# Score matmuls over 64 rows made 128 rows by zeroed key planes, in a two-layer DiT block on one NeuronCore

## The chip, the core and the metric

The kernel runs on one core of a Trainium2 chip. The metric is device time in microseconds for one execution, the median of three runs. The core has a matrix engine (TensorE, PE in the profile, with its weight loads listed apart as PEld), a vector engine (DVE), a scalar engine (ACT), a general engine (GpSimd, POOL) and queues that issue transfers (SP). Each takes its own instructions in its own order, and they meet through semaphores.

## The reference

Two layers act on 256 image tokens x and 256 context tokens. Each layer has a feed-forward block, a token mixing and a second feed-forward block, each with a norm ahead and behind and with shift, scale and gate from a condition vector. In the second layer the context no longer gets an output of its own. What matters here is the attention inside the token mixing: 8 heads of 64 channels, with the image queries looking at image keys (with a relative bias) and at context keys, and in layer 0 the context queries at context keys.

```python
def neighbourhood_attention(q, k, v, kc, vc, rpb, rows):
    ...
    s_loc = jnp.einsum('brqhd,brkchd->bhrqkc', q, k_blk, preferred_element_type=jnp.float32) * scale
    s_loc = jnp.where(col_valid[:, None, :], s_loc + bias, NEG_INF)
    s_ctx = jnp.einsum('brqhd,bkhd->bhrqk', q, kc, preferred_element_type=jnp.float32) * scale
    ...
    p = jax.nn.softmax(scores, axis=-1).astype(v.dtype)

def context_attention(q, k, v):
    ...
    sc = jnp.einsum('bqhd,bkhd->bhqk', q, k, preferred_element_type=jnp.float32) * dh ** -0.5
```

All inputs are float32, and so is the output.

## The kernel before, in words

**Precision.** Float32 is carried through the matrix engine in pairs: an upper part rounded to the engine's float32r and a lower part, the rest. A product is three matmuls, upper by upper, upper by lower and lower by upper (`mm3`). ACT makes the upper part by a copy, DVE the lower by a subtraction (`split`).

**Weights.** `Stream` loads raw float32 weights in blocks of 1 MB through two places (`raw`) and splits them into slots of the tag `big`, of which there are 16, each 8 KB a partition. The other tags are `wk` (10 work buffers), `ps` (the 8 PSUM banks) and `st` (small statistics).

**The order.** Nothing is issued as it is written. `Recorder` takes down every operation with its operands, gives each an estimated time (`price`), and `order` lays out all engines together: an operation can run once its operands are there and its new tiles have a place, and each engine takes the one that can start first, or of several the one taken down first. A tile gets a place only if one is left for each tile asked for before it. For a matmul of float32r the price depends on the number of columns alone (lines 212 to 216), not on the rows. `issue` then issues all of it from line 376, so that every instruction of the profile has that line; the views are read by tile names instead.

**The attention.** `token_mix` goes over four pairs of heads. For each, `k_part` and `q_part` project keys (`pk`) and queries (`pq`), with two heads side by side on the 128 partitions, head 0 on the first 64 and head 1 on the others (`HEADS`). `k_evac` and `q_evac` bring them to SBUF, the image part through the rotary embedding `roped`, whose tile is `rp` and in which POOL does one of the multiplications. `kb` has the keys in three planes: plane e holds head e's upper parts on both halves of the partitions, and plane 2 holds the lower parts of both heads, each on its own half. `qa` has the queries: plane e holds head e's upper part on its own half and its lower part on the other half.

So `scores` (lines 1006 to 1008) takes two matmuls per query tile of 128 tokens. The first, over 128 rows, gives upper by upper and lower by upper at once; the second, over the 64 rows of the head, adds upper by lower:

```python
mm(ps, qa[:, e, q0 : q0 + P], kb[:, e, ks], True, False)
mm(ps, qa[hp, e, q0 : q0 + P], kb[hp, 2, ks], False, True)
```

`head` runs it for two tiles of image queries against 512 keys (bank `pS`), and in layer 0 for two tiles of context queries against 256 keys (bank `pC`). DVE takes maxima, ACT the exponentials (`sx`, `sc`), PE transposes the probabilities (`pp`), ACT and DVE split them (`pT`), and PE multiplies them with the values `v` into `po`. Between these steps the planner sets projections (`pk`, `pq`, and `pu` of the pooling branch) and, at the end, the output projection `pd`. The pooling branch (`pooled`, tiles `U`, `dd`, `ds`, `py`) runs on POOL and ends in a small matmul.

Ahead of the attention stands the end of a feed-forward block: `close` squares and sums a token tile on ACT (`sq`, then `sx` for the next norm), POOL raises the sum to the power -1/2 (`power`, tile `rs`), and DVE and ACT go on with it.

Of the kernel before, what the change touches and what calls it, by code (L numbers as in the profile page):

```python
# [17 lines left out]
P = 128  # L18
# [27 lines left out]
class Buf:  # L46
    """A logical tile; it gets one of the places of its tag while the operations that use it run."""

# [7 lines left out]
class View:  # L56
    """A part of a logical tile, with the shape arithmetic that its operations need."""

# [61 lines left out]
    def extent(self):  # L120
        """(first partition, last partition, bits of the touched groups of 32 elements)"""
        base = View.BASES[self.buf.shape]
        width = base[0].size
        off = self.shadow.__array_interface__["data"][0] - base.__array_interface__["data"][0]
        key = (off, width, self.shadow.shape, self.shadow.strides)
        if key not in View.MASKS:
            p0, f0 = divmod(off, width)
            at = np.array([f0])
            for n, st in zip(self.shadow.shape[1:], self.shadow.strides[1:]):
                if st:  # L130
                    at = (at[:, None] + st * np.arange(n)[None]).reshape(-1)
            bits = 0
            for c in np.unique(at >> 5):
                bits |= 1 << int(c)
            View.MASKS[key] = (p0, p0 + self.shadow.shape[0] - 1, bits)
        return View.MASKS[key]
# [13 lines left out]
class DramView:  # L150
    """A part of a scratch tensor in DRAM; its operations are ordered as on the whole of it."""

# [24 lines left out]
class Recorder:  # L177
    """Takes down a program of operations, orders each engine's by estimated times, and issues them so.

    An operation runs when its operands are there and its new tiles have places; of those that could run,  # L180
    the one taken down first does. A tile gets a place only if one is left for each that was asked for
    before it, up to the tag's limit."""

# [99 lines left out]
    def lag(a, b, carries):  # L283
        """Time from the end of one operation to the start of another that needs it."""
        if a.engine == b.engine:
# [7 lines left out]
    def order(self):  # L293
# [15 lines left out]
        def room(op):  # L309
            """Earliest time at which the new tiles of the operation have places, or None."""  # L310
            at, taken = 0.0, {}
# [82 lines left out]
def tile_dit_block(  # L394
# [41 lines left out]

# [1 line left out]
    ident0 = pool.tile([P, P], F32, name="ident")  # L438
# [10 lines left out]

# [1 line left out]
    class Stream:  # L451
# [86 lines left out]

# [1 line left out]
    csil = fixed([P, KD, 2], "csil")  # L540
# [59 lines left out]
    def first_mod(j):  # L600
        """Scale or shift of the first norm, on the tensor engine."""
        pr = bank("pm")
# [70 lines left out]
    def fill(n):  # L673
        """Steps of the modulation vectors of later stages, behind the work around them."""
        debt[0] += n
        rec.delay = BEHIND
        while debt[0] >= 1 and todo:
            steps = todo[0][1]
            steps.pop(0)()
            debt[0] -= 1  # L680
            if not steps:
                todo.pop(0)
        rec.delay = 0
# [4 lines left out]

# [1 line left out]
    X = [fixed([P, D], f"x{t}") for t in range(4)]  # L690
# [10 lines left out]
    def power(sq, eps):  # L701
        """(sum of the two halves' mean squares + eps) ** -0.5"""
        st = stat(2, "rs")
# [12 lines left out]
    def unit(n, x, r):  # L716
        """n = x * r, the first half on one engine and the second on another."""
        nc.vector.tensor_scalar(out=n[:, HALVES[0]], in0=x[:, HALVES[0]], scalar1=r, scalar2=None, op0=ALU.mult)
# [9 lines left out]
    def normed(t, l, jshift, n, hf, Hn, sq):  # L728
        """h = modulate(rms_norm(x)) of one token tile, transposed and split."""
        shift, scale = cols[(l, jshift)], cols[(l, jshift + 1)]  # L730
# [16 lines left out]
    def first_unit(t):  # L747
        """Normed and transposed tile of the input, in PSUM."""
        n, sq = wtile([P, D], "n"), stat(2, "sq")
# [5 lines left out]
    def first_scale(v, pts):  # L755
        """Both tiles of a stream, times the scale."""
        hf = slot([P, KD, S], "hf", F32)
# [9 lines left out]
    def first_shift(v, hf, Hn):  # L767
        """The shift, and the split."""
        tk = slice(v * S, (v + 1) * S)
# [6 lines left out]
    def close(t, pd, y, half, nxt, Hn):  # L776
        """Residual update of one token tile from its product, then the next stage's norm (or the store)."""
        n = wtile([P, D], "n")
# [47 lines left out]

# [1 line left out]
    def ffn(l, ff, both, nxt, rate, lead, parts):  # L828
# [10 lines left out]
        def product(tt, pg, pu):  # L839
            """Twice silu(gate) * up."""  # L840
            nc.scalar.activation(tt[:, 0, :], pg, AF.Tanh, scale=0.5)
# [22 lines left out]
        def by_token():  # L864
            """The first tiles with the tokens as rows, one token tile after the other."""
            wb = [ws.get() for _ in range(KD)]
# [74 lines left out]

# [1 line left out]
    def token_mix(l, nxt):  # L943
# [28 lines left out]
        def k_evac(pk, kb):  # L972
            """For each of two heads, the upper part on both halves of the partitions; then the lower parts."""
            for cs, src in ((CS, pk[:, CS]), (XS, roped(pk, 1.0))):
                for e, hp in enumerate(HEADS):
                    nc.scalar.activation(kb[hp, e, cs], src[hp], AF.Copy)
                    nc.vector.tensor_sub(kb[hp, 2, cs], src[hp], kb[hp, e, cs])
                    nc.vector.tensor_copy(kb[HEADS[1 - e], e, cs], kb[hp, e, cs])

        def q_evac(pq, qa):  # L980
            """For each of two heads, the upper part on the head's half of the partitions, the lower on the other."""
            for e, hp in enumerate(HEADS):
# [17 lines left out]
        def head(pr, e, qk, bx):  # L1000
# [5 lines left out]
            def scores(ps, q0, ks):  # L1006
                mm(ps, qa[:, e, q0 : q0 + P], kb[:, e, ks], True, False)
                mm(ps, qa[hp, e, q0 : q0 + P], kb[hp, 2, ks], False, True)

# [133 lines left out]
        columns(pq, wq, XS)  # L1143
        qk = wtile([P, 2, N_TOK], "qa", F32R), slot([P, 3, N_TOK], "kb")
        k_evac(pk, qk[1])
# [26 lines left out]
        for pr in range(4):  # L1172
# [3 lines left out]
            if pr < 3:  # L1176
                qk = wtile([P, 2, N_TOK], "qa", F32R), slot([P, 3, N_TOK], "kb")
            head(pr, 0, now, bx)
# [36 lines left out]

# [1 line left out]
    nc.sync.dma_start(out=fold, in_=foldc)  # L1217
# [34 lines left out]
def _layout(inp):  # L1252
# [4 lines left out]
    def tiles(w, cols):  # L1257
        # [K, cols*n] -> [n, 128, (K/128)*cols]
        K, W = w.shape[-2:]
# [25 lines left out]

    # bias of the relative positions, laid out by query (row parity s, column j), head, row offset, key column
    W, KH, KW = 64, 8, 16
# [61 lines left out]
```

## Time and profile before

| what | value |
|---|---|
| median of 3 runs | 1707.25 us (1706.99, 1707.25, 1710.73) |
| profiled execution, span from first to last instruction | 1708.2 us (1708.239) |
| mean granted TensorE clock | 0.990 |
| PE busy | 1662.8 us, 97% |
| DVE busy | 1133.8 us, 66% |
| ACT busy | 684.6 us, 40% |
| POOL busy | 204.1 us, 12% |
| first and last score matmul | 459.8 us (layer 0), 1481.3 us (layer 1) |

The time of the profiled execution is given by its span; the timed runs are other executions. A row of the profile reads: line, engine, operation, the tile written and the tiles read (numbers left out), shape, count, then busy time and mean duration. `64*128` ahead of a shape is the part of the array that a matmul uses, rows by columns. A row of a timeline has its start and its length first, and in brackets the idle time of the engine ahead of it and what ended it.

### The profile page before, as it was taken

What the parts mean: (1) busy time and instruction counts of PE and PEld (TensorE: products, weight loads), DVE (VectorE), ACT (ScalarE), POOL (GpSimd) and SP (SyncE); (2) the same over time, 40 slices, a digit from 0 to 9 for tenths busy, and PEclk for the clock granted to TensorE, in tenths of its full rate; (3) what the DMA queues carried; (4) which work ended last, traced back from release to release, by engine and by line L of the source; (5) the groups of instructions that cost most, each with busy time, mean ns of one, the idle gap of its engine ahead of it and who ended that gap; (6) DMA issues with size and microseconds to landing.
All of it is one profiled execution on the core that took longest, in us unless ns stands there. A gap on an engine that the chain in (4) does not pass through costs nothing.

```text
span 1708.2 us, 21855 instructions
## 1 busy us (share of the span) xinstructions
PE 1662.8 (97%) x8384; PEld 1379.1 (81%) x8384; DVE 1133.8 (66%) x1610; ACT 684.6 (40%) x1216; POOL 204.1 (12%) x248
## 2 busy tenths in 40 slices
PE   6998999999999999999999999999999999999998
PEld 4986887888877689788888888888888888779997
DVE  7978774756678769876676387623343487976664
ACT  7423222235556562223123272232222266764442
POOL 1011111101121411111110021100000022210000
PEclk9999999999999899999999999999999999999999
DMA  9477655542221435765556337722332312246551
GB/s 377 167 180 243 225 197 139 201 166 81 87 73 41 152 110 198 234 210 197 150 184 239 119 118 257 242 99 76 105 118 97 105 63 101 100 173 208 206 199 66
DMA packets 109192, 268.99 MB, mean 157 GB/s; under 512 B 19745, under 2 KB 49569, under 8 KB 97313
## 3 DMA queue, kind: packets, MB, share of 16 engines
q1 hardware_dynamic: 109088, 267.60, 46.1%
q8 instruction: 66, 1.08, 0.3%
q14 instruction: 38, 0.30, 0.1%
HBM read 251.80 MB, written 1.09 MB: 148 GB/s over the span
## 4 chain that ended last, share of the span: by engine, by line
PE 79%; DVE 7%; DMA 6%; ACT 4%; POOL 2%; issue 1%; SPq 1%; POOLq 0%; DVEq 0%; ACTq 0%
PE pd_ps L376 24%; PE pu_ps L376 22%; PE pg_ps L376 21%; DMA wm_wk<-in_wmod_dram 3%; PE pk_ps L376 2%; PE pv_ps L376 2%; ACT n_wk L376 2%; PE pq_ps L376 2%; DVE acc_wk L376 2%; POOL rs_st L376 1%; DVE w_big L376 1%; PE pS_ps L376 1%; PE po_ps L376 1%; DMA w_big<-in_wmod_dram 1%; PE pt_ps L376 1%
## 5 line engine op out<-in xcount | busy, mean ns | idle before, releaser
L376 DVE TENSOR_TENSOR w_big<-raw_raw,w_big 128x1024 fp32r<-128x1024 f32 x312 | 388.4, 1258 | 153.0 <-ACT w_big L376 152.5
L376 PE MATMUL pu_ps<-h_big,w_big 128*128 128x512 f32 (+1 forms) x2400 | 476.8, 351 | 0.1
L376 PE MATMUL pg_ps<-h_big,w_big 128*128 128x512 f32 (+1 forms) x2208 | 441.5, 354 | 1.4 <-ACT h_big L376 1.4
L376 PEld LDWEIGHTS pu_ps<-h_big,w_big 128*128 128x128 f32 x2400 | 390.1, 188 | 63.8 <-DVE w_big L376 0.3
L376 ACT ACTIVATE w_big<-raw_raw 128x1024 fp32r<-128x1024 f32 x312 | 321.8, 1053 | 298.6 <-DMA raw_raw<-in_wgu_dram 126.1
L376 PE MATMUL pd_ps<-w_big,g_big 128*128 128x512 f32 x1848 | 433.1, 395 | 1.1 <-ACT g_big L376 0.7
L376 PEld LDWEIGHTS pd_ps<-w_big,g_big 128*128 128x128 f32 x1848 | 347.2, 189 | 81.1 <-ACT g_big L376 1.2
L376 PEld LDWEIGHTS pg_ps<-h_big,w_big 128*128 128x128 f32 x2208 | 362.6, 189 | 61.9 <-ACT h_big L376 1.7
L376 DVE SCALAR_TENSOR_TENSOR acc_wk<-wm_wk,csil,acc_wk 128x1024 f32<-128x1024 f32 x196 | 249.0, 1305 | 61.8 <-DMA wm_wk<-in_wmod_dram 61.7
L376 ACT ACTIVATE g_big<-tt_wk 128x512 fp32r<-128x512 f32 (+1 forms) x84 | 49.1, 584 | 365.2 <-DVE tt_wk L376 365.2
L376 POOL TENSOR_TENSOR part_wk<-part_wk 128x512 f32<-128x512 f32 (+2 forms) x84 | 92.6, 1103 | 551.2 <-DMA part_wk<-acc_wk 464.8
L376 DVE TENSOR_TENSOR tt_wk<-tt_wk,pu_ps 128x512 f32<-128x512 f32 (+1 forms) x86 | 53.9, 627 | 59.1 <-PE pu_ps L376 58.8
L376 DVE SCALAR_TENSOR_TENSOR tt_wk<-tt_wk,pg_ps 128x512 f32<-128x512 f32 (+1 forms) x86 | 53.9, 627 | 58.4 <-ACT tt_wk L376 57.7
L376 POOL TENSOR_SCALAR rs_st<-sq_st 128x1 f32<-128x1 f32 x24 | 7.7, 321 | 705.3 <-ACT n_wk L376 705.2
L376 ACT ACTIVATE tt_wk<-pg_ps 128x512 f32<-128x512 f32 (+1 forms) x86 | 47.0, 546 | 111.6 <-PE pg_ps L376 95.9
L376 DVE TENSOR_TENSOR g_big<-tt_wk,g_big 128x512 fp32r<-128x512 f32 (+1 forms) x84 | 55.1, 656 | 42.2 <-ACT g_big L376 42.2
L376 PE MATMUL pd_ps<-w_big,mix_big 128*128 128x512 f32 x288 | 73.1, 403 | 0.0
L376 DVE TENSOR_TENSOR y_big<-y_big,pd_ps 128x512 f32<-128x512 f32 x56 | 37.4, 683 | 42.3 <-PE pd_ps L376 42.3
L376 PEld LDWEIGHTS pd_ps<-w_big,mix_big 128*128 128x128 f32 x288 | 53.3, 191 | 12.2 <-issue 0.5
L376 DVE TENSOR_SCALAR acc_wk<-wm_wk,csil 128x1024 f32<-128x1024 f32 x28 | 21.1, 770 | 56.5 <-DMA wm_wk<-in_wmod_dram 56.5
L376 PE MATMUL pk_ps<-h_big,w_big 128*128 128x512 f32 (+1 forms) x240 | 50.3, 353 | 0.0
L376 PE MATMUL pv_ps<-w_big,h_big 128*128 128x512 f32 x192 | 46.8, 396 | 0.0
(132 smaller groups left out, 1240.6 us busy)
## 6 DMA issues: line engine op xcount, KB each, us to landing
raw_raw<-in_wgu_dram SPq DMA_DIRECT2D x84, 1024.0 KB, 4.9
wm_wk<-in_wmod_dram SPq DMA_DIRECT2D x128, 512.0 KB, 6.7
raw_raw<-in_wdn_dram SPq DMA_DIRECT2D x44, 1024.0 KB, 5.1
part_wk<-acc_wk SPq DMA_DIRECT2D x224, 64.0 KB, 2.8
raw_raw<-in_wkq_dram SPq DMA_DIRECT2D x8, 1024.0 KB, 4.8
raw_raw<-in_wout_dram SPq DMA_DIRECT2D x8, 1024.0 KB, 4.9
w_big<-in_wmod_dram SPq DMA_DIRECT2D x7, 1024.0 KB, 13.5
gb_wk<-grow SPq DMA_DIRECT2D x10, 512.0 KB, 6.0
```

The costliest lines, as they stand in the source:

```text
L376: getattr(getattr(nc, op.engine), op.method)(*[self.real(a) for a in op.args], **{k: self.real(a) for k, a in op.kw.items()})
```

## The change

The key tile gets a fourth plane. Plane 2 + e now holds the lower parts of head e alone, on that head's half of the partitions, and zeros on the other half. The zeros are written by POOL, two memsets of 64 partitions by 512 columns for each pair of heads. The second matmul of `scores` then takes all 128 rows of `qa`, whose other half meets the zeros, so the sum is what it was. The tile grows from 6 to 8 KB a partition, which is the size of a place of `big`. In the diff, comments and docstrings that were emptied are left out.

```diff
         def k_evac(pk, kb):
+            for e, hp in enumerate(HEADS):
+                nc.gpsimd.memset(kb[HEADS[1 - e], 2 + e, :].bitcast(F32), 0.0)
             for cs, src in ((CS, pk[:, CS]), (XS, roped(pk, 1.0))):
                 for e, hp in enumerate(HEADS):
                     nc.scalar.activation(kb[hp, e, cs], src[hp], AF.Copy)
-                    nc.vector.tensor_sub(kb[hp, 2, cs], src[hp], kb[hp, e, cs])
+                    nc.vector.tensor_sub(kb[hp, 2 + e, cs], src[hp], kb[hp, e, cs])
                     nc.vector.tensor_copy(kb[HEADS[1 - e], e, cs], kb[hp, e, cs])
...
             def scores(ps, q0, ks):
                 mm(ps, qa[:, e, q0 : q0 + P], kb[:, e, ks], True, False)
-                mm(ps, qa[hp, e, q0 : q0 + P], kb[hp, 2, ks], False, True)
+                mm(ps, qa[:, e, q0 : q0 + P], kb[:, 2 + e, ks], False, True)
...
-        qk = wtile([P, 2, N_TOK], "qa", F32R), slot([P, 3, N_TOK], "kb")
+        qk = wtile([P, 2, N_TOK], "qa", F32R), slot([P, 4, N_TOK], "kb")
```

The last pair of lines stands at two places, lines 1144 and 1177. There are two layers of four pairs, so sixteen memsets. A memset needs no operand, so the planner can set it as soon as its tile has a place.

**POOL, end of the first feed-forward block.** Before, POOL has the powers of the last two token tiles one behind the other (`rs`: `sq` for the residual, `sx` for the next norm), and then the rotary multiplications of the attention:

```order
L376 TENSOR_TENSOR rs_st_3163<-rs_st_3163,nhalf 128x1
L376 TENSOR_SCALAR rs_st_3216<-sx_st_3195 128x1
L376 TENSOR_TENSOR rs_st_3216<-rs_st_3216,nhalf 128x1
L376 TENSOR_SCALAR rs_st_3227<-sq_st_3189 128x1
L376 TENSOR_TENSOR rs_st_3227<-rs_st_3227,nhalf 128x1
L376 TENSOR_SCALAR rs_st_3274<-sx_st_3256 128x1
L376 TENSOR_TENSOR rs_st_3274<-rs_st_3274,nhalf 128x1
L376 TENSOR_TENSOR rp_wk_3419<-rp_wk_3419,ropet 128x256
```

The same place of the changed program has the zeroing of the first two key tiles of layer 0 between them:

```order
L376 TENSOR_TENSOR rs_st_3163<-rs_st_3163,nhalf 128x1
L376 MEMSET kb_big_3198 64x512 x2
L376 TENSOR_SCALAR rs_st_3219<-sx_st_3195 128x1
L376 TENSOR_TENSOR rs_st_3219<-rs_st_3219,nhalf 128x1
L376 TENSOR_SCALAR rs_st_3230<-sq_st_3189 128x1
L376 TENSOR_TENSOR rs_st_3230<-rs_st_3230,nhalf 128x1
L376 MEMSET kb_big_3243 64x512 x2
L376 TENSOR_SCALAR rs_st_3280<-sx_st_3262 128x1
L376 TENSOR_TENSOR rs_st_3280<-rs_st_3280,nhalf 128x1
L376 TENSOR_TENSOR rp_wk_3425<-rp_wk_3425,ropet 128x256
```

Two pairs of memsets now stand ahead of a power for the next norm; the rest of POOL keeps its order there, and the other two pairs of layer 0 come further on, among the rotary and pooling steps.

**PE, first head of layer 0.** Before, the scores stand behind the values' projection `pv` and ahead of the next pair's keys `pk`:

```order
L376 MATMUL pv_ps_3499<-w_big_2983,h_big_3129 128x512
L376 MATMUL pS_ps_3536<-kb_big_3427,qa_wk_3460 128x512 x2
L376 MATMUL pS_ps_3540<-kb_big_3427,qa_wk_3460 128x512 x2
L376 MATMUL pC_ps_3546<-kb_big_3427,qa_wk_3460 128x256 x4
L376 MATMUL pk_ps_3552<-h_big_3132,w_big_3236 128x512
```

The changed program has, in the same rows of PE:

```order
L376 MATMUL pv_ps_3504<-w_big_2983,h_big_3129 128x512
L376 MATMUL pS_ps_3541<-kb_big_3198,qa_wk_3465 128x512 x2
L376 MATMUL pS_ps_3545<-kb_big_3198,qa_wk_3465 128x512 x2
L376 MATMUL pC_ps_3551<-kb_big_3198,qa_wk_3465 128x256 x4
L376 MATMUL pk_ps_3557<-h_big_3132,w_big_3239 128x512
```

Nothing has moved: in all of layer 0 PE, ACT, DVE and SP keep the order of their rows (the shape printed is that of the result, so the rows of the array that a matmul takes are not seen in it).

**POOL, pooling branch of layer 1.** Before, the steps of the second pooling group (`dd`, from `U`) follow one another:

```order
L376 TENSOR_TENSOR dd_wk_10956<-U_wk_10928 128x319
L376 TENSOR_TENSOR dd_wk_10967<-dd_wk_10956 128x317
L376 TENSOR_TENSOR dd_wk_10956<-dd_wk_10967,U_wk_10928 128x256
L376 TENSOR_TENSOR dd_wk_10956<-dd_wk_10956,U_wk_10928 128x256
L376 TENSOR_TENSOR rp_wk_11088<-rp_wk_11088,ropet 128x256
```

Now the last key tile of the layer is zeroed between them:

```order
L376 TENSOR_TENSOR dd_wk_10971<-U_wk_10943 128x319
L376 TENSOR_TENSOR dd_wk_10982<-dd_wk_10971 128x317
L376 MEMSET kb_big_10995 64x512
L376 TENSOR_TENSOR dd_wk_10971<-dd_wk_10982,U_wk_10943 128x256
L376 MEMSET kb_big_10995 64x512
L376 TENSOR_TENSOR dd_wk_10971<-dd_wk_10971,U_wk_10943 128x256
L376 TENSOR_TENSOR rp_wk_11117<-rp_wk_11117,ropet 128x256
```

The last two steps of that group stand behind a memset each. From here on the planner's order differs on PE, ACT and DVE too, in the second half of layer 1's attention and, by a row here and there, behind it.

More of the change, by code (lines that the diff above doesn't have):

```diff
@@ L1176, in token_mix @@
             if pr < 3:
-                qk = wtile([P, 2, N_TOK], "qa", F32R), slot([P, 3, N_TOK], "kb")
+                qk = wtile([P, 2, N_TOK], "qa", F32R), slot([P, 4, N_TOK], "kb")
             head(pr, 0, now, bx)
```

## The prediction

> **What bounds the kernel now.** I read the page first: which engine is full, and what the chain that ended last is made of.
>
> ```profile
> span 1708.2 us, 21855 instructions
> PE 1662.8 (97%) x8384; PEld 1379.1 (81%) x8384; DVE 1133.8 (66%) x1610; ACT 684.6 (40%) x1216; POOL 204.1 (12%) x248
> PE 79%; DVE 7%; DMA 6%; ACT 4%; POOL 2%; issue 1%; SPq 1%; POOLq 0%; DVEq 0%; ACTq 0%
> ```
>
> PE, the TensorE, is busy for 97% of the span and makes up 79% of the chain. So what shortens PE's own work counts, as long as nothing else is late instead. The change touches only the score products, so the second view is the one of the tile pS (scores of the token queries) and of pC (those of the context queries): how many of them there are, and in which shapes.
>
> ```profile
> L376 PE MATMUL pS_ps<-kb_big,qa_wk x64: 389/498/794, 459.8 to 1481.3; 128*128 128x512 f32 x32, 64*128 64x512 f32 x32
> L376 PE MATMUL pC_ps<-kb_big,qa_wk x32: 275/382/581, 461.4 to 567.9; 128*128 128x256 f32 x16, 64*128 64x256 f32 x16
> ```
>
> Half of the 96 score products run over 64 rows, 32 + 16 = 48, each recorded right behind a 128-row one. The ends of matmuls are modelled, so durations (498 ns) do not give the price; starts do. The third view is the timeline of PE, then of its weight loads, at the first head of the first layer.
>
> ```profile
> 457.42 2.50 PE L376 MATMUL pv_ps<-w_big,h_big 128*128 128x512 f32 x10
> 459.75 1.67 PE L376 MATMUL pS_ps<-kb_big,qa_wk 128*128 128x512 f32 x4
> 461.36 1.32 PE L376 MATMUL pC_ps<-kb_big,qa_wk 128*128 128x256 f32 x4
> 462.61 5.13 PE L376 MATMUL pk_ps<-h_big,w_big 128*128 128x512 f32 x21
> 467.57 0.60 PE L376 MATMUL pp_ps<-ident,sc_wk 128*128 128x128 f32 x4
> ...
> 474.06 1.46 PE L376 MATMUL po_ps<-pT_big,v_big 128*128 128x256 f32 x11
> 475.35 2.03 PE L376 MATMUL pq_ps<-h_big,w_big 128*128 128x512 f32 x8
> ```
>
> ```profile
> 459.53 0.19 PEld L376 LDWEIGHTS pS_ps<-kb_big,qa_wk 128*128 128x128 f32 x1
> 460.08 0.18 PEld L376 LDWEIGHTS pS_ps<-kb_big,qa_wk 64*128 64x128 f32 x1 [0.36 <-issue]
> ...
> 460.93 0.18 PEld L376 LDWEIGHTS pS_ps<-kb_big,qa_wk 64*128 64x128 f32 x1 [0.25 <-issue]
> ```
>
> From start to start, ten 128-row products of 512 columns take (459.75 - 457.42)/10 = 0.233 us each, and eleven of 256 columns (475.35 - 474.06)/11 = 0.117 us. The eight score products take 462.61 - 459.75 = 2.86 us, where 4 x 0.233 + 4 x 0.117 = 1.40 would do; the 21 behind them take 4.96 instead of 4.89. The four 64-row products thus cost 1.46 + 0.07 = 1.53 us, **0.38 us each**. The loads show where it lies: the first, 128 rows on 128, starts 0.22 us ahead of its product at 459.75; the two of 64 rows wait 0.36 and 0.25 us on nothing but issue, and start with their product instead of ahead of it.
>
> **The chain in the two attention stages.** PE does not bound all of this stretch, so I read who was on the chain (the pieces of the chain in order of time, one layer after the other), and the busy times of those stretches.
>
> ```profile
> 505.95 0.61 ACT pT_big L376
> 511.06 0.44 PE pp_ps L376 x2
> 543.91 0.71 ACT sx_wk L376
> 561.40 5.83 PE pS_ps L376 x8
> 1427.08 0.38 ACT mix_big L376
> 1478.49 1.94 PE pS_ps L376 x5
> ```
>
> ```profile
> 459.70:511.00 51.30, 50.64 (x244) 37.83 (x243) 38.32 (x102) 29.23 (x79) 12.23 (x15) 1.00 0.24 78
> 511.00:543.40 32.40, 32.34 (x156) 24.71 (x157) 26.27 (x77) 20.99 (x59) 2.79 (x4) 1.00 0.12 37
> 543.40:561.30 17.90, 14.91 (x82) 12.29 (x81) 17.14 (x27) 11.68 (x22) 8.53 (x7) 1.00 0.26 101
> 561.30:568.40 7.10, 7.00 (x12) 3.08 (x12) 3.50 (x8) 1.97 (x5) 1.95 (x3) 0.50 0.52 171
> 1413.00:1427.00 14.00, 14.00 (x76) 10.76 (x74) 8.33 (x30) 6.60 (x19) 0.73 (x1) 1.00 0.33 116
> 1427.00:1478.00 51.00, 48.95 (x318) 41.28 (x317) 46.53 (x119) 37.45 (x92) 16.11 (x20) 1.00 0.24 84
> 1478.00:1484.00 6.00, 6.00 (x25) 3.69 (x24) 5.94 (x18) 3.99 (x7) 3.79 (x5) 1.00 0.22 89
> ```
>
> The columns of the second view are length, then PE, its loads, DVE, ACT, POOL, then the granted clock. Layer 0: PE is on the chain up to 505.95 and from 511.06 to 543.4; from 543.9 to 561.4 ACT and DVE are (DVE busy 17.14 of 17.90); then PE at half clock. Layer 1: PE up to 1427; to 1478 DVE is full to 46.53 of 51.00. The stall before it is seen on PE's timeline, in the bracket:
>
> ```profile
> 561.40 5.83 PE L376 MATMUL pS_ps<-kb_big,qa_wk 128*128 128x512 f32 x8 [3.09 <-DVE qa_wk L376]
> 567.03 1.43 PE L376 MATMUL pC_ps<-kb_big,qa_wk 64*128 64x256 f32 x3
> 568.40 2.93 PE L376 MATMUL pd_ps<-w_big,mix_big 128*128 128x512 f32 x6
> 571.12 0.57 PE L376 MATMUL py_ps<-ds_wk,wp_wk 128*128 128x512 f32 x1
> ```
>
> **Part 1: 48 products go from 64 to 128 rows.** No product is added, and each still streams 512 or 256 columns. The bound is 48 x 0.38 = 18.2 us. What of it reaches the end goes by stretch; half of the scores in each of the seven windows are of 64 rows, 16, 8, 2 and 6 in layer 0 and 4, 8 and 4 in layer 1. The counts are those of the same windows for pS and pC alone, of which the first and the last for pS stand here (as many pC in the first, none in layer 1).
>
> ```profile
> 459.70:511.00 51.30, 6.74 (x16) 1.00 0.24 78
> ...
> 1478.00:1484.00 6.00, 3.46 (x8) 1.00 0.22 89
> ```
>
> From 459.7 to 511 it is 16 x 0.38 = 6.1 us. DVE idles 51.3 - 38.3 = 13.0 us there, so it can follow; PE is not on the chain for the 5.1 us from 505.95 to 511.06, and I take 1 us off for that: 5.1. From 511 to 543.4 it is 8 x 0.38 = 3.0 us; DVE idles 6.1 us, and I take two thirds: 2.0. From 543.4 to 561.3 there are 2, but PE arrives early anyway and waits 3.09 us for qa: 0.
>
> From 561.4 to 568.4 eight pS and three pC at half clock take 568.40 - 561.40 = 7.0 us. The pd products behind them take (571.12 - 568.40)/6 = 0.45 us each at that clock, so 8 x 0.45 + 3 x 0.22 = 4.3 would do, and the chain lies on PE: 2.7. Layer 0 comes to 9.8.
>
> In layer 1 it is 4 x 0.38 = 1.5 us on PE's own chain before 1427, and I take all of it. Of the 8 x 0.38 = 3.0 from 1427 to 1478 I leave 0.5, since DVE has but 4.5 us of idle time there, and of the 1.5 after 1478 I leave 1.0, DVE being full (5.94 of 6.00). Layer 1 comes to 3.0.
>
> Together 9.8 + 3.0 = 12.8 us.
>
> **Part 2: sixteen memsets on POOL.** The nearest row is the zeroing of U:
>
> ```profile
> L376 POOL MEMSET U_wk<- x8: 584/592/602, 470.4 to 1473.8; 128x592 f32 x8
> ```
>
> The gaps that it has around the places of the first memsets stand in its timeline, in brackets:
>
> ```profile
> 426.30 0.80 POOL L376 TENSOR_SCALAR rs_st<-sx_st 128x1 f32<-128x1 f32 x1 [4.42 <-ACT n_wk L376]
> 432.00 1.35 POOL L376 TENSOR_SCALAR rs_st<-sx_st 128x1 f32<-128x1 f32 x1 [3.27 <-ACT n_wk L376]
> 446.49 0.74 POOL L376 TENSOR_TENSOR rp_wk<-rp_wk,ropet 128x256 f32<-128x256 f32 x1 [12.50 <-ACT rp_wk L376]
> ```
>
> 592 ns for 592 columns, so about 0.51 us for 512 and 1.0 us per pair of heads. The first two pairs are queued ahead of the second norm's square root, for which DVE and ACT wait, and each waits until PE has let go of a place of the tag big. Both fall into POOL's idle gaps of 4.42 and 3.27 us, which hide them as long as that place comes free within some 2 us of the gap's start; without that cover it is 1 us each. The others in layer 0 stand in gaps like the 12.50 us one. Bounds 0 to 2 us a layer, with no gain possible, since it is work added; I take 0. The second 64-row product's new wait for POOL is over long before: 426 against 459.75.
>
> **Part 3: the order.** In layer 0 PE, ACT, DVE and SP keep their rows. In layer 1 the last pair's two memsets stand between two steps of the pooling, 0.5 us each ahead of ds and py, and from there PE, DVE and ACT are laid out anew. No row of before prices that; the two longest waits of PE in layer 1's attention bound it:
>
> ```profile
> PE pp_ps L376 <- DVE sx_wk L376: 1.1, 3, 0.5
> PE pS_ps L376 <- DVE qa_wk L376: 0.4, 1, 0.4
> ```
>
> 1.5 us, and some tenths of smaller ones, is all that a luckier order could win. As much, or twice that, it may lose, so -2 to +3 us; I take +1, since the memsets push ds back by 1 us. **Sum**: 1708.2 - 12.8 + 1 = 1696.4 us for the profiled span. The median of the timed runs, 1707.25, lies 1.0 us under that span, so 1695.4 us.
>
> **A rule that speaks against the change.** The page shows PE and its loads busy for 1662.8 + 1379.1 us in a span of 1708.2, so loads of 128 rows do run under products of 128 rows; the one at 459.53 ended before its own product began at 459.75, while pv ran. Were the padded loads bare all the same, 0.19 us (the row at 459.53) behind each of the 48 would take 9.1 us off the 18.2, and in proportion half off the 12.8: 6.4 us, so 1702. I give that 2%. The Trainium skill, "TensorE: Matmul & The Clock Gate", Part 3, The mechanism, has in its list of what overlaps that a weight load runs under other matmuls only where its row groups differ. By that rule it is this case; the trace does not agree.
>
> **The rivals.** *All of it arrives* (14%): DVE follows everywhere and the stall before 561.4 is no longer than now. 18.2 us: 1689. For it: DVE's idle 13.0 and 6.1 us in layer 0. Were the half clock gone too, the work from 561.4 to 571.1 would run in half the time, some 4 us less: 1685, a third of this case.
>
> *DVE takes it* (14%): only PE's own stretch ahead of 511 and that before 1427 give, halved by waits of the softmax chain: (6.1 + 1.5)/2 = 3.8, so 1703. For it: DVE at 91 to 99% of three of the seven windows. Against it: its queue in layer 0 starts earlier too.
>
> *It is not the height* (3%): the 0.38 us belongs to the accumulating second product, and stays: 1707. Against it: every other accumulating product keeps to 0.233 us.
>
> *The clock* (5%): slower. PE's work shrinks, the DVE chain does not, and the stall grows. A stall of 3.09 us was followed by half clock up to 571.1 at least (the 0.45 us of pd), some 10 us in which PE lost 5 us of work; 3.1 + 5 = 8 us a stall. The place is layer 1 from 1448 to 1478, laid out anew with DVE full. One new stall over 3 us leaves 4 us of the gain; from two on it is lost: 1695.4 + 16 = 1711. The Trainium skill, "TensorE: Matmul & The Clock Gate", HAM oscillation, has the clock fall after a wholly idle window of about 3.4 us. By that alone I would give this rival 3%; in this trace 3.09 us was enough.
>
> **How the numbers follow.** The forecast, 62%, has its own range from 1690 to 1702 (term bounds: 3 us of part 1's cuts, 4 of POOL, 3 of order). With the rivals the range is 1687 to 1703: it leaves out the clock (5%), the useless change (3%), half of the second rival (7%) and the third of the first one in which the half clock goes too (5%). A measurement can tell about 0.2%, 3.4 us, from no change. Faster: 62 + 14 + 2 and most of 14, so 0.89; same: 3 and a little of the third case, 0.06; slower: 0.05.
>
> **What would show it.** Right: the 64x512 and 64x256 forms are gone, and from the first pS to the first pk of the first head it is 1.4 us, not 2.86; the load rows lose their waits on issue. PE's wait for qa, now the one that ends at 561.4, grows to 4 or 5 us and the half clock stays. Wrong: score products that still start over 0.3 us apart at full clock; or a PE that waits for DVE by 12 us more in the two attentions; or a norm's square root on POOL held behind a memset.

## The result and the profile after

| kernel | median us | runs | range us |
|---|---|---|---|
| before | 1707.86 | 4 | 1706.99 to 1710.73 |
| after | 1694.9 | 4 | 1693.02 to 1697.12 |

The ratio is 0.9921, 95% interval 0.9907 to 0.9935: 13.0 us faster, with 1695.4 forecast. The profiled execution of after took 1693.02 us, the shortest of its four, and has a span of 1691.2 us. So 1.8 us lie around a span, and the profiled execution of before (span 1708.2) must have taken some 1710 us, near the upper end of its runs. The two profiles therefore differ by 17.0 us, 4 us more than the medians; below, stretches of the profiles are compared, not their spans.

The page of after, its engines:

```profile
span 1691.2 us, 21873 instructions
PE 1640.4 (97%) x8384; PEld 1377.1 (81%) x8384; DVE 1134.6 (67%) x1610; ACT 684.9 (40%) x1216; POOL 216.8 (13%) x264
```

PE still has its 8384 products, but 22 us less busy time; the 16 memsets raise POOL from 248 to 264 instructions and make up 16 x 0.52 = 8.3 of its 12.7 us more. The groups of the tile kb show what became of the products, and what a memset takes:

```profile
L376 PE MATMUL pS_ps<-kb_big,qa_wk x64: 388/396/767, 458.2 to 1459.2; 128*128 128x512 f32 x64
L376 PE MATMUL pC_ps<-kb_big,qa_wk x32: 275/280/415, 459.1 to 555.7; 128*128 128x256 f32 x32
...
L376 POOL MEMSET kb_big<- x16: 518/520/523, 420.6 to 1422.3; 64x512 f32 x16
```

The forms of 64 rows are gone; a memset takes 520 ns, where 0.51 us had been estimated. PE's timeline, at the first head of layer 0 and at the stall for the last pair's queries, and then the loads of that first head:

```profile
458.20 1.09 PE L376 MATMUL pS_ps<-kb_big,qa_wk 128*128 128x512 f32 x4
459.13 0.64 PE L376 MATMUL pC_ps<-kb_big,qa_wk 128*128 128x256 f32 x4
459.61 5.01 PE L376 MATMUL pk_ps<-h_big,w_big 128*128 128x512 f32 x21
...
551.73 3.75 PE L376 MATMUL pS_ps<-kb_big,qa_wk 128*128 128x512 f32 x8 [3.88 <-DVE qa_wk L376]
555.28 0.84 PE L376 MATMUL pC_ps<-kb_big,qa_wk 128*128 128x256 f32 x3
555.92 2.40 PE L376 MATMUL pd_ps<-w_big,mix_big 128*128 128x512 f32 x6
```

```profile
457.98 0.88 PEld L376 LDWEIGHTS pS_ps<-kb_big,qa_wk 128*128 128x128 f32 x4
```

From the first pS to the first pk it is 459.61 - 458.20 = 1.41 us, where it was 2.86; four products of 512 columns start 0.93/4 = 0.233 us apart. The loads stand in one row of four with no wait in it, and start 0.22 us ahead of their products. At the stall the wait for qa is 3.88 us instead of 3.09. The windows of after, cut at the same products as the first four of before, and one of layer 1 (columns as before):

```profile
458.15:504.45 46.30, 44.77 (x244) 37.10 (x243) 37.84 (x102) 29.14 (x79) 13.20 (x17) 1.00 0.26 86
504.45:533.75 29.30, 29.26 (x156) 24.44 (x157) 25.52 (x76) 20.85 (x60) 3.05 (x4) 1.00 0.09 29
533.75:551.70 17.95, 14.10 (x82) 12.09 (x81) 17.18 (x27) 11.67 (x22) 8.61 (x7) 0.98 0.33 121
551.70:555.90 4.20, 4.17 (x11) 3.43 (x12) 3.42 (x8) 1.97 (x5) 1.87 (x3) 0.50 0.84 289
1409.00:1457.00 48.00, 43.70 (x299) 38.90 (x297) 43.54 (x114) 34.94 (x86) 14.04 (x18) 1.00 0.25 89
```

The four of layer 0 were 51.30, 32.40, 17.90 and 7.10 us long: they lose 5.0, 3.1, 0.0 and 2.9 us, 11.0 together. In layer 1 PE now idles more: 48.00 - 43.70 = 4.3 us in the fifth window, where it was 51.00 - 48.95 = 2.1, while DVE is as full as it was (the order of the products differs there, so the two windows do not hold quite the same work). Who makes PE wait from 1385 to 1545 (us in total, times, the longest):

```profile
PE pg_ps L376 <- ACT h_big L376: 2.7, 1, 2.7
PE py_ps L376 <- DVE ds_wk L376: 2.5, 2, 1.4
PE pS_ps L376 <- DVE qa_wk L376: 1.8, 2, 1.3
PE pp_ps L376 <- DVE sx_wk L376: 1.2, 3, 0.5
```

The first of them was 2.1 us long in before, at the norm behind the attention; ds and qa made PE wait 0.3 and 0.4 us there. Last, POOL's timeline at the first memsets:

```profile
420.60 1.10 POOL L376 MEMSET kb_big<- 64x512 f32 x2 [0.35 <-POOL rs_st L376]
424.75 0.80 POOL L376 TENSOR_SCALAR rs_st<-sx_st 128x1 f32<-128x1 f32 x1 [3.05 <-ACT n_wk L376]
...
430.52 1.27 POOL L376 TENSOR_SCALAR rs_st<-sx_st 128x1 f32<-128x1 f32 x1 [2.20 <-ACT n_wk L376]
```

The square root behind each pair of memsets still waits for ACT, 3.05 and 2.20 us (4.42 and 3.27 before): the memsets lie in those gaps and hold nothing up.

### The profile page after: what moved, and what is told of

The parts are those of the page before. It is cut to its first block, busy times and chain, and to the rows that moved or that the text cites. A ratio compares the mean times of both kernels' runs of the same rounds, so it can differ in the third digit from the quotient of the medians.

```text
span 1691.2 us, 21873 instructions
## 1 busy us (share of the span) xinstructions
PE 1640.4 (97%) x8384; PEld 1377.1 (81%) x8384; DVE 1134.6 (67%) x1610; ACT 684.9 (40%) x1216; POOL 216.8 (13%) x264
## 4 chain that ended last, share of the span: by engine, by line
PE 78%; DVE 7%; ACT 5%; DMA 4%; POOL 2%; issue 2%; SPq 1%; POOLq 0%; DVEq 0%; ACTq 0%
PE pd_ps L376 25%; PE pu_ps L376 22%; PE pg_ps L376 22%; PE pk_ps L376 2%; DMA wm_wk<-in_wmod_dram 2%; PE pv_ps L376 2%; ACT n_wk L376 2%; DVE w_big L376 2%; POOL rs_st L376 1%; DVE acc_wk L376 1%; PE pq_ps L376 1%; SPq L376 1%; DMA w_big<-in_wmod_dram 1%; PE pt_ps L376 1%; DMA part_wk<-acc_wk 1%
## 5 line engine op out<-in xcount | busy, mean ns | idle before, releaser
L376 POOL TENSOR_TENSOR part_wk<-part_wk 128x512 f32<-128x512 f32 (+2 forms) x84 | 95.8, 1140 | 539.4 <-DMA part_wk<-acc_wk 432.4
```

The costliest lines, as they stand in the source:

```text
L376: getattr(getattr(nc, op.engine), op.method)(*[self.real(a) for a in op.args], **{k: self.real(a) for k, a in op.kw.items()})
```

## The experiments

All kernels with their times; ratios are to the kernel before on the same chip (1708.15, 1707.33 and 1706.79 us in the three rounds of runs; its own 20 runs of the second go from 1701.3 to 1713.4, so one run alone says little, but layer 1 of an unchanged order repeats within 0.1 us from trace to trace). The last two columns are read from PE's timeline of each profile: layer 0 from the first pS to the third group of transposes (`pt`) for the norm behind it, at 629.05 us in before, and layer 1 from its first pS to the first pg of the feed-forward block behind it.

| kernel | median us | ratio, 95% interval | layer 0 us | layer 1 us |
|---|---|---|---|---|
| before | 1707.86 | | 169.3 | 99.3 |
| after | 1694.9 | 0.9921 (0.9907 to 0.9935) | 158.4 | 98.8 |
| e1, before again | 1708.5 (one run) | | 169.2 | 99.3 |
| e2, layer 0 alone | 1694.68 | 0.9922 (0.9905 to 0.9939) | 158.4 | 99.4 |
| e3, layer 1 alone | 1708.55 | 0.9994 (0.9980 to 1.0009) | 169.4 | 98.9 |
| e4, grouped heights | 1703.91 (one run) | | 161.7 | 100.2 |
| e5, memsets unpriced | 1692.6 | 0.9905 (0.9888 to 0.9921) | 157.7 | 98.7 |
| e6, before, short maximum | 1705.64 | 0.9993 (0.9979 to 1.0008) | 168.1 | 99.1 |
| e7, e5 with short maximum | 1690.27 | 0.9904 (0.9888 to 0.9919) | 156.3 | 97.0 |
| e8, e5 with later pooling | 1701.28 | 0.9968 (0.9953 to 0.9983) | 160.7 | 98.7 |
| e9, e5 with queries first | 1684.01 | 0.9863 (0.9845 to 0.9882) | 152.5 | 95.8 |
| e10, before, queries first | 1700.55 | 0.9956 (0.9940 to 0.9972) | 163.4 | 98.6 |

**What a 64-row product pays for (e4).** The kernel before, with the products of a head's image queries in another order (two small helpers of the edit are written out here; the context queries stay as they were):

```python
for t in range(2):
    pS.append(bank("pS"))
    mm(pS[t], qa[:, e, t * P : t * P + P], kb[:, e, ALL], True, False)
for t in range(2):
    mm(pS[t], qa[hp, e, t * P : t * P + P], kb[hp, 2, ALL], False, True)
```

> The kernel before (64-row products kept), but for each head's image queries both 128-row products come first and both 64-row products behind them, in place of tall, low, tall, low. Theory (what costs is the change of the row count, some 0.38 us for going down and coming back): one such change per head in place of two, so from the first pS to the first pC of the first head it is 4 x 0.233 + 0.3 to 0.4 = 1.2 to 1.35 us, where the kernel before has 1.61. Rival (each 64-row or second, accumulating product costs the 0.38 us by itself): 1.6 us again. The total may fall by up to 16 x 0.38 = 6 us by the theory, less what DVE takes; one run can't show that within 3 us.

PE's timeline at the first head:

```profile
457.98 1.29 PE L376 MATMUL pS_ps<-kb_big,qa_wk 128*128 128x512 f32 x4
459.20 1.32 PE L376 MATMUL pC_ps<-kb_big,qa_wk 128*128 128x256 f32 x4
460.45 0.73 PE L376 MATMUL pk_ps<-h_big,w_big 128*128 128x512 f32 x2
```

```profile
457.75 0.42 PEld L376 LDWEIGHTS pS_ps<-kb_big,qa_wk 128*128 128x128 f32 x2
458.54 0.29 PEld L376 LDWEIGHTS pS_ps<-kb_big,qa_wk 64*128 64x128 f32 x2 [0.36 <-issue]
459.20 1.12 PEld L376 LDWEIGHTS pC_ps<-kb_big,qa_wk 128*128 128x128 f32 x4 [0.37 <-issue]
```

The four take 459.20 - 457.98 = 1.22 us, as the theory has it, and not 1.6. The whole group, up to the first pk, takes 460.45 - 457.98 = 2.47 us: 1.07 over the 1.40 of plain spacing, for six changes between the two heights (two in pS, four in pC). In before it was 1.46 for eight. That is 0.18 us a change in both kernels, or some 0.36 us down to 64 rows and back; with the 0.07 us that the pk products behind the group take longer in before it is the 0.38 of the prediction. The second of two 64-row products in a row adds nothing to that, so neither the 64 rows nor the accumulating second product costs anything; the change between two heights does.

The loads (second view) fit the price. A load takes 0.18 to 0.19 us. The first 64-row load starts at 458.54, with its product and not ahead of it, and so does the 128-row one at 459.20; both wait on nothing but issue. The second 64-row load lies inside the 0.29 us of that row, and its product starts at 458.88, behind it. So a load runs under the product before it where both have one height, and stands bare at a change. Why it can't be loaded ahead there, the trace does not say. The Trainium skill, "TensorEngine Tiling (Array Packing)", Key Properties, says that a change of the tiling mode drains the TensorE; the trace agrees that the change costs, 0.18 us each way. The change under study takes away both changes of all 48 products.

The total (one run) and layer 0's 161.7 us are not to be read as the price of the heights: PE's wait for qa before the last pair is 1.2 us here, no half clock follows it, and one of 6.8 us stands in layer 1, from 1468.7.

**Which layer gives it (e1, e2, e3).** The memsets and 128-row products in one layer only (the key tile keeps its four planes in both), and the kernel before once more. The edit of e2; e3 has `not full` in place of `full`:

```diff
-            for e, hp in enumerate(HEADS):
-                nc.gpsimd.memset(kb[HEADS[1 - e], 2 + e, :].bitcast(F32), 0.0)
+            if full:
+                for e, hp in enumerate(HEADS):
+                    nc.gpsimd.memset(kb[HEADS[1 - e], 2 + e, :].bitcast(F32), 0.0)
...
-                mm(ps, qa[:, e, q0 : q0 + P], kb[:, 2 + e, ks], False, True)
+                if full:
+                    mm(ps, qa[:, e, q0 : q0 + P], kb[:, 2 + e, ks], False, True)
+                else:
+                    mm(ps, qa[hp, e, q0 : q0 + P], kb[hp, 2, ks], False, True)
```

> The kernel before, unchanged, for a second trace of it. The two profiled spans differ by 17.0 us, the timed medians by 13.0, and 5 us of the 17 lie in the feed-forward blocks between the attentions, which the change does not touch. If that part is chance (my theory), this span lies 1 to 4 us under 1708.2, and the waits of PE for the summed modulation rows (1.3 us at 705 and 2.3 us at 1065 in the first trace) come out otherwise, while layer 0's attention is as long as it was within 0.5 us. If the change brought it there (rival), this trace repeats 1708 within 1 us, with both waits as long.

> The padded planes in layer 0 alone; layer 1 keeps its 64-row products, and PE, DVE, ACT and SP keep the order of before throughout. My theory, by the terms of the prediction: 9.8 us under before, ratio 0.994. Rival, read off the two traces (layer 0's attention shrank by 10.9 us, layer 1's kept nothing): all of the measured 13 us, ratio 0.9924. Rival that DVE takes it: under 4 us.

> The padded planes in layer 1 alone, with layer 1's order as in the changed kernel. My theory: 3.0 us of products less 1 us for the new order, so 2 us under before, ratio 0.999. Rival, from the traces, where layer 1 was 3.5 us ahead in the middle and 0 at the end: no gain, ratio 1.000. Rival that all arrives: 6 us, 0.9965.

Layer 0 alone gives all of it (0.9922), layer 1 alone nothing that can be measured (0.9994). The interval of e3 would still hold the 2 us that were forecast for layer 1; its profile, 99.3 - 98.9 = 0.4 us, does not. The layer that is not changed keeps its length, 169.4 and 99.4 us. So the total of the prediction came out right over a split that did not, and that is luck. The span of e1 is 1706.7 us, 1.5 under that of before, and the two waits of PE for the modulation rows are 0.9 and 1.0 us in place of 1.3 and 2.3, as the theory of chance has it.

**The planner's price (e5).** One line, by which the planner counts the memsets at nothing; all engines then keep their order of before in both layers, apart from the memsets themselves:

```diff
-                return 0.03 + size / 1200.0
+                return 0.0 if outs[0].buf.name == "kb" else 0.03 + size / 1200.0
```

> The whole change, with the planner told that a memset of the key tile takes no time; PE, DVE, ACT and SP then keep the order of before in both layers. It tells the price of the new order apart from that of the products. My theory: 1 us faster than the changed kernel, so 14 us under before, ratio 0.992. If the new order is what ate layer 1's gain: 3 us faster than the changed kernel, 0.9905. If DVE ate it in either order: as the changed kernel, 0.9924.

1692.6 us is 2.3 us under after, but the intervals of the two ratios overlap, and layer 1 is as long with the old order (98.7 us) as with the new one (98.8). What takes layer 1's gain is not the new order.

**Where layer 1's gain goes (e6, e7).** From the first pS of layer 1 to the last, before takes 67.96 us, after 63.30 and e5 66.07; from there to the first pg it is 31.33, 35.51 and 32.62. The order of after has 12 products behind the last pS that before has ahead of it, so e5, in the order of before, is the one to compare. It wins 1.6 us by the ninth pS, 1.9 us by the last, and is left with 0.6 at the first pg. The stretches from the ninth pS to the last, before and then e5:

```profile
1436.34:1481.34 45.00, 43.15 (x254) 34.15 (x253) 41.62 (x108) 32.05 (x80) 14.41 (x18) 1.00 0.31 107
1418.65:1463.34 44.69, 39.03 (x255) 34.22 (x254) 41.02 (x106) 30.89 (x79) 14.19 (x19) 1.00 0.30 107
```

PE needs 4.1 us less, and idles 5.7 us instead of 1.9; DVE is busy for 92% of both. To see whether DVE takes it, DVE got less to do, in the same order: the shift of the softmax is the maximum over all image keys and the first 8 context keys, in place of all 256, and that of the context queries the one over their first 8 keys. In the planner both keep their old price.

```diff
-                nc.vector.reduce_max(st[:, 2 + t : 3 + t], pS[t][:, CS], axis=AX.X)
+                nc.vector.reduce_max(st[:, 2 + t : 3 + t], pS[t][:, S : S + 8], axis=AX.X)
...
-                nc.vector.reduce_max(sm[:, 0:2], pCv, axis=AX.X)
+                nc.vector.reduce_max(sm[:, 0:2], pCv[:, :, 0:8], axis=AX.X)
```

> A control: the kernel before, in its own order, with less work on DVE. The softmax's maximum is taken over the first 8 context keys only, in place of 256 (the shift is then another one, 32 reductions of 0.41 us and 8 of 0.69 us shrink to some 0.15 us, so DVE loses about 12 us of work, 4 us of it in layer 1). If DVE bounds parts of the attention in the kernel before: 2 to 6 us faster. If PE bounds all but the stall: within 2 us.

> The padded kernel with unpriced memsets (order of before everywhere) and the same short maximum. It is compared with the short maximum in the kernel before. Theory (layer 1's gain on PE was taken by DVE, which is over 90% busy there): with 4 us less DVE work in layer 1 its attention is at least 2.5 us shorter than in the control, and the total differs by 17.5 us or more from the control, in place of 15.5. Rival (the gain is lost to the fixed order and its waits for transfers and ACT, not to DVE's amount of work): layer 1's attention within 1 us of the control's, total difference 14 to 16 us.

The kernel before gains nothing measurable by it (0.9993; by the profiles 1.2 us in layer 0 and 0.2 in layer 1), as expected where PE bounds all but the stall. With 128 rows layer 1 is 99.1 - 97.0 = 2.1 us shorter than the control, where e5 had kept 0.6 us. That lies between the two expectations (at least 2.5, and within 1). The totals differ by 1705.64 - 1690.27 = 15.4 us, as much as by e5 without the edit and short of the theory's 17.5, though the two intervals are too wide to exclude that. PE's three longest waits for DVE in layer 1 of e7:

```profile
PE pp_ps L378 <- DVE sx_wk L378: 1.9, 3, 1.3
PE py_ps L378 <- DVE ds_wk L378: 1.6, 2, 1.4
PE pu_ps L378 <- DVE w_big L378: 0.6, 1, 0.6
```

In e5 these three are 2.0, 1.6 and 1.6 us. So the amount of DVE's work takes a part of the gain; the waits for sx and ds stay. That they are the ends of chains which DVE goes through step by step, and which less work hardly shortens, is an argument and not shown. A part may be what the next experiment finds in layer 0: in after the two subtractions into qa at 1456.31, right ahead of PE's longest wait for qa in layer 1 (1.34 us), take 1.75 us beside additions of POOL, where e8 has a pair of the same form in 0.87.

**What the stall is made of (e8).** In e5 the wait of PE for qa is 3.88 us, as in after. These are DVE's steps ahead of it, and POOL's additions beside them, one by one:

```profile
546.55 0.78 DVE L376 TENSOR_SCALAR sc_st<-sc_st 128x2 f32<-128x2 f32 x1
547.24 0.41 DVE L376 TENSOR_TENSOR rp_wk<-rp_wk,ropet 128x256 f32<-128x256 f32 x1
547.58 2.18 DVE L376 TENSOR_TENSOR w_big<-raw_raw,w_big 128x1024 fp32r<-128x1024 f32 x1
549.69 1.38 DVE L376 TENSOR_TENSOR rp_wk<-rp_wk 128x256 f32<-128x256 f32 x1
550.99 1.74 DVE L376 TENSOR_TENSOR w_big<-raw_raw,w_big 128x1024 fp32r<-128x1024 f32 x1
552.76 0.83 DVE L376 TENSOR_TENSOR qa_wk<-rp_wk,qa_wk 64x256 fp32r<-64x256 f32 x1
```

```profile
546.13 1.18 POOL L376 TENSOR_TENSOR dd_wk<-U_wk 128x591 f32<-128x591 f32 x1
547.38 1.30 POOL L376 TENSOR_TENSOR dd_wk<-dd_wk 128x589 f32<-128x589 f32 x1
548.76 2.02 POOL L376 TENSOR_TENSOR dd_wk<-dd_wk 128x585 f32<-128x585 f32 x1
550.86 0.78 POOL L376 TENSOR_TENSOR dd_wk<-dd_wk,U_wk 128x256 f32<-128x256 f32 x1
551.61 1.70 POOL L376 TENSOR_TENSOR dd_wk<-dd_wk,U_wk 128x256 f32<-128x256 f32 x1
```

The step of 547.24 starts as one addition is about to end, at 547.31, and ahead of the next; it runs in 0.41 us. The others start under an addition and take 1.4 to 5 times as long as in e8 below. In e8 a copy of one column on POOL reads the last pair's queries, so that the pooling additions come behind them (from there on the planner also lays out PE, DVE and ACT anew):

```diff
             src, lo, hi = U, 0, n
+            if full and g == 2:
+                nc.gpsimd.tensor_copy(pair[0][:, 0:1], qa[:, 1, S - 1 : S].bitcast(F32))
```

> The padded kernel with unpriced memsets, and in layer 0 the third pair's pooling additions on POOL wait for the last pair's queries (one more 128x1 copy on POOL reads qa). In the padded kernel PE waits 3.9 us for qa, and beside these additions DVE's steps take 2.18, 1.38, 1.74 and 0.85 us in place of 1.23, 0.42, 1.23 and 0.42. Theory (POOL's additions stretch DVE's steps, and that is the wait): the steps ahead of qa are back at their short times, PE's wait for qa falls to under 1.5 us and the half clock behind it goes; 3 to 5 us from that, against which the pooling and what hangs on it comes 3 to 5 us later: total within 1690 to 1695. Rival (DVE's queue alone sets it): steps as long as now, the wait stays at 3.5 to 4 us, and the later pooling makes it 2 to 4 us slower than 1692.6.

The same steps of DVE, and then PE at the last pair:

```profile
548.12 0.15 DVE L376 TENSOR_SCALAR sc_st<-sc_st 128x2 f32<-128x2 f32 x1
548.26 0.43 DVE L376 TENSOR_TENSOR rp_wk<-rp_wk,ropet 128x256 f32<-128x256 f32 x1
548.60 1.22 DVE L376 TENSOR_TENSOR w_big<-raw_raw,w_big 128x1024 fp32r<-128x1024 f32 x1
549.74 0.42 DVE L376 TENSOR_TENSOR rp_wk<-rp_wk 128x256 f32<-128x256 f32 x1
550.07 1.22 DVE L376 TENSOR_TENSOR w_big<-raw_raw,w_big 128x1024 fp32r<-128x1024 f32 x1
551.32 0.42 DVE L376 TENSOR_TENSOR qa_wk<-rp_wk,qa_wk 64x256 fp32r<-64x256 f32 x1
```

```profile
551.89 1.39 PE L376 MATMUL pS_ps<-kb_big,qa_wk 128*128 128x512 f32 x5 [0.46 <-DVE qa_wk L376]
```

The cause of the stall is shown: without POOL's additions the steps are back at 0.15, 1.22, 0.42, 1.22 and 0.42 us. From the 128x2 step to the end of the first qa it is 551.74 - 548.12 = 3.62 us, where e5 has 553.59 - 546.55 = 7.04; that is 3.42 us, and PE's wait falls by as much, from 3.88 to 0.46.

The ends tell more than the lengths. In e5 the additions end at 547.31, 548.68, 550.78, 551.64 and 553.31, and the five stretched steps at 547.33, 549.76, 551.07, 552.73 and 553.59: each its own short length, less 0.13 to 0.14 us, behind the addition under which it began. So a step does not run slowly beside an addition; it waits for its end. The Trainium skill, "SBUF — State Buffer", Who interferes with whom, has it that a DVE instruction with two SBUF inputs contends with a GpSimd instruction that reads SBUF, and that the port pair they share is an exclusive lock. The trace agrees: four of the five have two inputs in SBUF. But the 128x2 step has only one and waits too (0.78 us for 0.15), so two inputs are not the condition.

The total is a miss: 1701.28, not 1690 to 1695. The wait came back behind the stall. The additions now run there, and DVE's steps beside them are stretched in turn: three subtractions of 128x1024 from 558.03 take 5.09 us together, where three of 1.22 would be 3.66. PE's waits from 553 to 600:

```profile
PE pd_ps L376 <- ACT sx_wk L376: 3.0, 2, 1.7
PE py_ps L376 <- DVE pT_wk L376: 2.1, 1, 2.1
PE pp_ps L376 <- ACT sx_wk L376: 1.1, 1, 1.1
```

They are 6.2 us, and the clock was granted at half for 10.2 us from 560.7, so layer 0 takes 160.7 us, 3.0 more than in e5.

**The stall taken away another way (e9, e10).** Instead of holding the pooling back, the queries come earlier: their rotary part is recorded first, and the planner gives their steps a head start. All else is e5; e10 has the same edit in the kernel before.

```diff
+            src = roped(pq, 0.125)
             for e, hp in enumerate(HEADS):
                 if full:
...
-            src = roped(pq, 0.125)
...
+            rec.haste = 0.5
             q_evac(pq, qk[0])
+            rec.haste = 0.0
```

> The padded kernel with unpriced memsets, and the queries are brought to SBUF with their rotary part recorded first and with a head start of 0.5 us in the planner. In the last pair of layer 0 all of qa's steps then stand on DVE ahead of the third pair's pooling additions on POOL, and the pooling is not held back. Theory (the 3.9 us wait is DVE's steps stretched beside POOL's additions, and the half clock follows from the wait): the wait for qa is gone or under 1 us, no half clock around 550 to 560, and the total falls by 3.9 + 1.7 = some 5 us against the 1692.6 of the kernel without this edit: 1686 to 1689. Rival (PE then waits for something else in that place, as with the later pooling): within 2 us of 1692.6.

> The control of the run above: the same edit of the query steps in the kernel before, with its 64-row products. If the stall costs the same without the padding (3.1 us of wait, 10 us of half clock behind it, together 3.1 + 5 = 8 us): 1699 to 1702. The padding is then worth the difference to the run above, 13 to 15 us if the two edits add up, less if the padding's gain was in part the shortened half clock.

PE's waits in layer 0 of e9 (440 to 640), and its window behind the place of the stall:

```profile
PE pp_ps L376 <- DVE sm_st L376: 1.6, 2, 1.2
PE pp_ps L376 <- DVE sc_wk L376: 1.5, 2, 1.0
...
PE pC_ps L376 <- DVE qa_wk L376: 0.2, 1, 0.2
```

```profile
550.00:640.00 90.00, 87.47 (x540) 76.52 (x541) 71.26 (x110) 53.15 (x112) 19.65 (x24) 1.00 0.37 135
```

The wait for qa is 0.2 us, the clock stays at 1.00, and the kernel takes 1684.01 us, 0.9863 (0.9845 to 0.9882): faster than both kernels under study, and under the 1686 to 1689 that was expected. Layer 0 is 157.7 - 152.5 = 5.2 us shorter than in e5, the 5 us of the theory; another 98.7 - 95.8 = 2.9 us comes in layer 1, where all query steps are earlier too. The control e10 took 1700.55 us, within its 1699 to 1702. Against it the padding is worth 1700.55 - 1684.01 = 16.5 us by the medians, above the 13 to 15 expected, but by the two profiled executions it is 1695.4 - 1681.6 = 13.8 us, and these are placed: 10.9 us in layer 0 and 98.6 - 95.8 = 2.8 us in layer 1. The two kernels have one order on PE, DVE and ACT. With the queries early layer 1 keeps what it lost in after.

## Why the prediction was right, and where it was not

**The price of 0.38 us a product** was right: 1.41 us from pS to pk, with 1.4 forecast, and e4 shows it to be the two changes of height, 0.18 us each and some. The rival that the accumulating product costs it is out by e4. So is the bare load: products 0.233 us apart leave no room for a load of 0.19 us between them. It is at a change of height that the load stands bare, so it was the products of before that paid it.

**Layer 0** was forecast at 5.1 + 2.0 + 0 + 2.7 = 9.8 us and gave 5.0 + 3.1 + 0 + 2.9 = 11.0 (10.9 to the end of the stage). The first, third and fourth term hold to 0.2 us. The second was mis-sized: I left a third of the 3.0 us to DVE, and all of it arrived; DVE's idle time there went from 6.1 to 29.30 - 25.52 = 3.8 us, so it was enough. As forecast, PE's wait for qa grew (3.88 us; 4 to 5 was said, so just under it) and the half clock stayed; it lasted 6.8 us from 550.9, where it had been 10.2 us. In e5 the same wait of 3.88 us was followed by only 3.4 us of it; what sets its length stays open.

**Layer 1** was forecast at 3.0 - 1 = 2.0 us and gave 0.5 by the profile, and by e3's time nothing that can be told from none. The step that failed is the end of part 1, "I leave 0.5" for 1427 to 1478 and "of the 1.5 after 1478 I leave 1.0", in a sum in which nothing is lost behind them. The 1.5 us before 1427 did arrive: from layer 1's first pS to its ninth, behind that place, it is 21.38 us in after and 22.96 in before. But in the order of before (e5) the twelve 64-row products behind that gave 0.3 us and not 1.5 by the last pS, and then 1.3 us were lost up to the first pg, as PE idled longer in both stretches. In after PE was 4.7 us ahead at the last pS, in part because 12 products had moved behind it, and 4.2 us of that went behind it: to those products, and as PE idled 35.51 - 30.81 = 4.7 us there instead of 2.1, for mix, ds and the norm. Part 3's +1 us for the new order has nothing to show for it: with the old order layer 1 is as long (e5). What took the gain was waits for DVE, as the second rival had it, but in layer 1 alone; by e7 the amount of DVE's work is a part of the cause, and the rest stays open.

**The base.** Taking 1.0 us off between the span and the median was chance in one profile: 1.8 us lie around a span, and that execution was longer than the median. The sum of 12.8 - 1 = 11.8 us was thus set against 13.0 us measured. The attentions account for 10.9 + 0.5 = 11.4 us of these; the other 1.6 us are not placed. The long stretch between the two takes 784.3 us in before and 779.3 in after, but with 64-row products it also takes 781.1 (e1), 785.9 (e4) and 779.0 us (e10). Whether the padding saves anything there stays open.

**The stall** was put down to DVE being full, 17.14 of 17.90 us. It was full, but 3.9 us of that were steps waiting for POOL (in before 0.77, 2.19, 1.38, 1.74 and 1.70 us, the last for two, where e8 has 0.15, 1.22, 0.42, 1.22 and 0.87). This changed no term of the sum; it hid the 5 us that e9 found. The clock's rival did not come: no new wait reached 3 us, and no new half clock came. POOL's memsets cost nothing, as forecast.

## What to carry to other kernels

On a PE that is full, count changes between products of different heights, not the rows: where a half-height product stands between full ones, as here, zero rows cost less than the two changes, and where that can't be had, put products of one height side by side. What PE wins reaches the end only where the engine it next waits for has finished early; read that from the waits at the end of the stage, not from the share of idle time in a window. A busy engine can be busy because its steps wait for another one: compare one instruction's time inside the stall with the same form elsewhere, and its end with the ends on the other engine, before taking the work as given.

## What was not expected of the hardware

- A DVE subtraction of 128x1024 with both inputs in SBUF took 1.22 us alone and up to 2.18 us beside POOL's additions, one of 128x256 0.42 and 1.38 us, and even a step of 128x2 with one input 0.15 and 0.78 us: each ended its own short length, less 0.13 to 0.14 us, behind the addition. Who starts first is not held: the subtraction at 544.34 in e5 took 1.22 us, and POOL's product that began under it, at 544.86, 1.31 us where e9 has 0.75. Reductions out of PSUM kept their time (0.69 us for 128x512 at 545.60 in e5, with POOL busy).
- Taking 3.9 us of PE's wait away gave 5.2 us in layer 0, since the 3.4 us of half clock behind it went too.
- A second 64-row product right behind another costs no more than a 128-row one, and a change of height costs 0.18 us, about one weight load (e4: 1.07 us for six changes).
- Half clock needs no single wait of 3 us. In the 3.41 us before it set in, PE was still busy for 0.47 us in before (from 561.25), 1.28 us in e8 (from 560.73) and 1.75 us in e4 (from 1468.67), where its longest wait was 1.4 us.
